# Twelve of sixteen macro tiles as a loop of six turns, and other shares of the copies, in a rotation of an 8192 x 8192 matrix

## The chip, the cores and the metric

The kernel runs on one NeuronCore of a Trainium2 chip. The metric is the device time of one execution in microseconds (us). Before the change the median of three runs is 1258.31 us (1258.22 to 1258.31).

The core has five engines with instruction streams of their own: TensorE (PE in the profile; PEld is its weight load), VectorE (DVE), ScalarE (ACT), GpSimd (POOL) and SyncE (SP). They meet through semaphores. Data moves between the chip's main memory (HBM) and the on-chip memory (SBUF, 128 partitions) on 16 DMA engines, which all queues share. TensorE writes to a second on-chip memory, PSUM, from which ScalarE copies here.

## The reference

```python
def setup_inputs():
    return {"x": np.random.randn(8192, 8192).astype(np.float32), "k": 1}

def reference(x, k):
    return np.rot90(x, k)
```

With k = 1 this is out[8191 - c, r] = x[r, c]: a transposition with the order of the columns reversed. Every one of the 67,108,864 values is read once and written once, 268.4 MB each way, and nothing is calculated.

## The kernel before

**Tiles.** x is cut into KK = 16 macro tiles of R = 1024 rows and W = 4096 columns. A macro tile comes in as T = 8 loads of 128 rows x 4096 columns (2 MB, 16 KB to a partition). It goes out as J = 8 outputs of 512 rows of the result x 1024 columns (2 MB). So there are 128 loads m, counted through, and 128 outputs n = 8 kk + j. A load consists of 8 chunks of 128 x 512, one for each output; output j needs chunk j of all eight loads of its macro tile.

**Buffers.** There are five buffers of 128 x 4096: LAND = 2 for loads, OUTS = 3 in which outputs are put together. The first five loads go to all five at once. Between them lies `ring`, with 63 chunk slots (SLOTS): a chunk of the next macro tile is written where an output of the present one has just been read. Therefore VectorE may take load m only when output m - 8 has been read from the ring. The 64th chunk of a macro tile, the corner, has no slot: it is turned around inside its landing buffer (L354), transposed by TensorE (L393) and copied by ScalarE (L433).

**Two ways to make an output.** Which outputs go which way is said by `by_pe(kk)` (L84): all eight in the first and last macro tile, j = 0 and 4 (BY_PE) in macro tiles 1 to 13, and five in macro tile 14.
- By TensorE: VectorE copies the chunk into the ring with its columns reversed (L359, COPY). TensorE transposes 32 blocks of 128 x 128 into two PSUM halves (L407), and ScalarE copies these into the output buffer (L449).
- By quadrants: VectorE's 32 x 32 block transpose writes the chunk into the ring (L359, STREAM_TRANSPOSE). Each 32 x 32 block then still has to go to another group of 32 partitions. Since an engine's copy takes one group of 32 partitions to one other, an output takes 16 copies of 32 x 1024 (`moves`, L245). BY_DVE = 1 of the 16 is made by VectorE (L341), BY_POOL = 9 by GpSimd (L324), the other 6 by ScalarE (L430 and L439). GpSimd's last copies wait until ScalarE and VectorE have made theirs, and ScalarE then waits for GpSimd.

**Order.** Each engine's whole program is written out by hand, with the waits, by a function: `by_gpsimd` (L303), `by_sync` (L327), `by_vector` (L331), `by_tensor` (L372), `by_scalar` (L416). Everything is unrolled.
- SyncE issues the loads (three and four halves of the first ten are ScalarE's), each when its landing buffer has been taken.
- For load m VectorE first makes its copy for output m - 8, if that goes by quadrants; then it waits for the landing and for output m - 8; then it takes the chunks.
- ScalarE goes through the outputs in order of n. It makes its part, waits for the others' and issues the store (L457). So a late output also holds the store of the next one.
- `room_for(wait, n)` (L180) waits until the last store from the buffer of output n has landed. Before the change that buffer is the one of output n - 3 (`out_buf`, L161).

Of the kernel before, what the change touches and what calls it, by code (L numbers as in the profile page):

```python
# [6 lines left out]
P = 128  # L7
# [6 lines left out]
J = W // (G * P)  # L14
# [5 lines left out]
SLOTS = T * J - 1  # L20

Q = 32
BY_DVE = 1
BY_POOL = 9
BY_PE = [0, 4]
EARLY = range(T + 2)
BOTH = EARLY[-4:]

# [3 lines left out]
LAND = 2  # L32
OUTS = 3

LINE = 1024
HEAD = 224


def whole_reads(nc):

    for fn in nc.m.functions:
        for block in fn.blocks:
            for n, ins in enumerate(block.instructions):
                if not isinstance(ins, mybir.InstDMACopy):
                    continue
                src = ins.ins[0]
                ap = [list(d) for d in src.ap]
                if len(ap) == 3 and ap[2][0] == 1 and ap[1][0] == ap[2][1]:
                    ap = [ap[0], [1, 1], [1, ap[1][1] * ap[2][1]]]
                    block.instructions[n] = copy.replace(  # L50
                        ins,
                        ins=[copy.replace(src, ap=ap)],
                        ant_dge_precooked=False,
                    )


def slot(kk, t, j):
# [4 lines left out]
def kernel(tc: tile.TileContext, x: bass.AP, k: bass.AP, out: bass.AP):  # L62
    nc = tc.nc
# [6 lines left out]
    KK = len(macros)  # L70
# [26 lines left out]
    for n, (kk, ts, js, blocks) in enumerate(outs):  # L97
        if moved[n]:
            continue
        rows = len(ts) * P  # L100
# [25 lines left out]
    def moved_until(n):  # L126
        return sum(moved[: n + 1])
# [28 lines left out]
    def load_buf(m):  # L156
        if m < T:
            return m % (LAND + OUTS)
        return LAND + 2 if m == T else (m - T - 1) % LAND

    def out_buf(n):  # L161
        e = n - (KK * J - J)
        if e < 0:
            return LAND + (n + 1) % OUTS
        ends = [load_buf(n_load - 2)]
        ends += [LAND + (KK * J - J + i + 1) % OUTS for i in range(OUTS)]
        ends += [load_buf(n_load - 1)]
        return ends[e % len(ends)]

    def once(e):  # L170
        seen = {}

        def wait(sem, n):
            if seen.get(sem, 0) < n:
                seen[sem] = n
                e.wait_ge(sem, n)

        return wait
# [33 lines left out]
    for m in range(n_load):  # L212
        kk, t = divmod(m, T)
# [49 lines left out]

    pairs = [(a, q) for a in range(P // Q) for q in range(P // Q)]

    def load(e, m):
        r0, c0 = macros[m // T]
        b = load_buf(m)
        rows = slice(0, P)
        if m in BOTH:  # L270
            rows = slice(0 if e is nc.sync else 1, P, 2)
        r = r0 + m % T * P
        e.dma_start(  # L273
            out=bufs[b][rows, :], in_=x[r : r + P, c0 : c0 + W][rows, :]
        ).then_inc(s_land[b], 16)

    def queues(m):
        if m in BOTH:
            return [nc.sync, nc.scalar]
        return [nc.scalar if m in EARLY and m % 2 else nc.sync]  # L280

    def load_in_turn(e, m):
        if e not in queues(m):
            return
        last = [i for i in range(m) if load_buf(i) == load_buf(m)]
        taken(e.wait_ge, last[-1])
        load(e, m)

    def landings(m):
        return 16 * sum(1 + (i in BOTH) for i in range(m + 1) if load_buf(i) == load_buf(m))  # L290
# [5 lines left out]
    with tc.tile_critical():  # L296
        for m in range(LAND + OUTS):
            for e in queues(m):
                load(e, m)
    tc.close()  # L300
    tc.compile()  # L301

    def by_gpsimd(e):  # L303
        e.memset(ident, 0.0).then_inc(s_id, 1)  # L304
        e.wait_ge(s_id, 1)
        e.affine_select(  # L306
            out=ident,
            in_=ident,
            compare_op=mybir.AluOpType.not_equal,
            fill=1.0,  # L310
            base=0,
            pattern=[[-1, P]],
            channel_multiplier=1,
        ).then_inc(s_id, 1)
        wait = once(e)
        for n, (kk, _, js, _) in enumerate(outs):
            if moved[n]:
                room_for(wait, n)
                wait(s_rev, turned_in(n))
                others = {BY_POOL - 2: s_act, BY_POOL - 1: s_dve}  # L320
                for c, (to, of) in enumerate(moves(n, pairs[BY_DVE : BY_DVE + BY_POOL])):
                    if c in others:
                        wait(others[c], moved_until(n))
                    i = e.tensor_copy(out=to, in_=of)  # L324
                i.then_inc(s_pool, 1)

    def by_sync(e):  # L327
        for m in range(LAND + OUTS, n_load):
            load_in_turn(e, m)

    def by_vector(e):  # L331
        wait = once(e)
        for m in range(n_load):
            kk, t = divmod(m, T)
            b = load_buf(m)
            n = m - T
            if n >= 0 and moved[n]:
                room_for(wait, n)
                wait(s_rev, turned_in(n))
                for to, of in moves(n, pairs[:BY_DVE]):  # L340
                    i = e.tensor_copy(out=to, in_=of)  # L341
                i.then_inc(s_dve, 1)
            e.wait_ge(s_land[b], landings(m))
            if n >= 0:
                if moved[n]:
                    e.wait_ge(s_pool, moved_until(n))  # L346
                else:
                    e.wait_ge(s_half, turned_until(n))
            for js in pieces[m]:
                if (m, js[0]) == (n_load - 1, J - 1):  # L350
                    e.wait_ge(s_half, turned_until(KK * J - J))
                if kk < KK - 1 and (t, js[0]) == (T - 1, J - 1):
                    wait(s_rev, rev[m, 0])
                    e.tensor_copy(  # L354
                        out=at(bufs[b][:], 0, [[CH, 1], [1, CH]]), in_=landed(b, js)
                    ).then_inc(s_rev, 1)
                    continue
                turn = e.transpose if in_quadrants(kk, js[0]) else e.tensor_copy
                turn(out=chunk(kk, t, js), in_=landed(b, js)).then_inc(s_rev, 1)  # L359
# [10 lines left out]
                yield n, parts[n]  # L370

    def by_tensor(e):  # L372
        wait = once(e)
        e.wait_ge(s_id, 2)
        used = {}
        for n, some in in_turn():
            kk, ts, js, blocks = outs[n]
            rows = len(ts) * P
            order = [(part, f) for part in some for f in part[2]]
            if js[0] == 0 and kk < KK - 1:  # L380
# [33 lines left out]
                    used[h] = part  # L414

    def by_scalar(e):  # L416
        wait = once(e)
        e.wait_ge(s_id, 2)
        e.copy(scratch, ident[:, :1])  # L419
        for m in EARLY[LAND + OUTS :]:  # L420
            load_in_turn(e, m)
        for n, (kk, ts, js, blocks) in enumerate(outs):
            r0, c0 = macros[kk]
            rows = len(ts) * P
            b = out_buf(n)
# [16 lines left out]
            else:  # L442
                for k, h, cols in parts[n]:
# [11 lines left out]
            top = M - c0 - js[0] * CH - groups * P  # L455
            left = r0 + ts[0] * P
            e.dma_start(  # L457
                out=out[top : top + groups * P, left : left + rows].rearrange(
                    "(g m) f -> m g f", m=P
                ),  # L460
                in_=bufs[b][:, : groups * rows].rearrange("m (g f) -> m g f", f=rows),
            ).then_inc(s_store[b], 16)

    by_gpsimd(nc.gpsimd)
    by_sync(nc.sync)
    by_vector(nc.vector)
    by_tensor(nc.tensor)
    by_scalar(nc.scalar)

    last = {out_buf(n): n for n in range(n_out)}  # L470
    for b in sorted(last, key=last.get):
# [36 lines left out]
```

## Time and profile before

| what | before |
|---|---|
| median of three runs | 1258.31 us |
| span of the profiled execution (its own time, first to last instruction) | 1256.9 us |
| busy: TensorE / VectorE / ScalarE / GpSimd | 330.0 / 612.7 / 682.5 / 805.0 us |
| GpSimd's copies L324 | 729, 804.3 us |
| ScalarE's copies of quadrants L430 and L439 | 486, 497.7 us |
| VectorE's copies of quadrants L341 | 81, 108.0 us |
| transposes on TensorE L407 and L393 | 1,556 |
| moved by DMA, HBM read and written | 537.22 MB, 268.44 and 268.44 MB |
| mean rate over the span | 427 GB/s |
| a macro tile in the middle of the span | 78.1 us |

The span is that of one profiled execution; the runs' times include what lies around it. Lines such as L324 are lines of the kernel's file. In a row of the groups of instructions stand the line, the engine, the operation, what is written and read with partitions x elements, the count, the busy time and the mean of one in ns, and then the idle time of the engine ahead of these instructions with what ended it. In the DMA queue rows stand packets, MB, and the time of the packets as a share of 16 engines' span; the queues called "instruction" carry the engines' code. A row of the table of stretches has for each of the five engine columns the busy us and the number of instructions, then TensorE's granted clock, the mean share of the 16 DMA engines that was busy, and the rate.

### The profile page before, as it was taken

The numbers are of one execution on the slowest core, as the hardware profiler recorded it, in microseconds if no ns is written. First come the engines' busy times: TensorE is split into PE (matmuls) and PEld (weight loads), VectorE is DVE, ScalarE is ACT, GpSimd is POOL, SyncE is SP. The second block draws the span as 40 slices with busy tenths as digits, with TensorE's granted clock in tenths as the row PEclk, the third lists the DMA queues.
The fourth block names the chain that finished last, engine by engine and source line by source line (L and its number), as shares of the span: only waits on it lengthen the run. The fifth ranks groups of instructions, "written<-read, shape, count | busy, mean of one in ns | idle before, by whom it ended". The sixth has DMA issues, their size and how long they took to land.

```text
span 1256.9 us, 5389 instructions
## 1 busy us (share of the span) xinstructions
PE 330.0 (26%) x1556; PEld 267.9 (21%) x1556; DVE 612.7 (49%) x373; ACT 682.5 (54%) x637; POOL 805.0 (64%) x735
## 2 busy tenths in 40 slices
PE   1555122221122211222212322023220232214374
PEld 0444111211112110121201212012120121103364
DVE  2544554556545555455555555555555555453310
ACT  0334565565555655566555555556555655556454
POOL 0000886768867679677797767977678776795500
PEclk9987555555555555565555555555555555555588
DMA  9999999999999999999999999999999999999999
GB/s 398 420 431 428 430 428 430 430 430 430 428 429 430 430 429 428 430 429 430 429 430 429 430 427 431 430 430 429 430 429 430 429 429 429 429 430 429 430 426 394
DMA packets 36957, 537.22 MB, mean 427 GB/s; under 512 B 4160, under 2 KB 4160, under 8 KB 4160
## 3 DMA queue, kind: packets, MB, share of 16 engines
q10 hardware_dynamic: 19184, 278.93, 52.2%
q1 hardware_dynamic: 17744, 257.96, 48.0%
q8 instruction: 12, 0.20, 0.1%
q14 instruction: 17, 0.14, 0.0%
HBM read 268.44 MB, written 268.44 MB: 427 GB/s over the span
## 4 chain that ended last, share of the span: by engine, by line
DMA 72%; DVE 16%; POOL 5%; ACT 3%; issue 2%; PE 1%; ACTq 0%; SPq 0%; DVEq 0%
DMA buf<-in_x_dram 65%; DVE ring L359 16%; DMA out_dram<-buf 7%; POOL buf L324 5%; ACT buf L449 3%; PE ps L407 1%; ACTq L457 0%; DVE buf L341 0%; PE ps L393 0%; SPq L273 0%; DVE buf L354 0%; DVEq L346 0%; SPq L301 0%; SPq L193 0%; SPq L296 0%
## 5 line engine op out<-in xcount | busy, mean ns | idle before, releaser
L324 POOL COPY buf<-ring 32x1024 f32<-32x1024 f32 (+1 forms) x729 | 804.3, 1103 | 380.3 <-DMA out_dram<-buf 343.4
L407 PE MATMUL ps<-head,ring 128*128 128x128 f32 x1496 | 316.8, 384 | 880.6 <-DVE ring L359 430.3
L407 PEld LDWEIGHTS ps<-head,ring 128*128 128x128 f32 x1496 | 257.6, 200 | 936.9 <-DVE ring L359 435.0
L359 DVE COPY ring<-buf 128x1024 f32<-128x1024 f32 (+5 forms) x152 | 158.1, 1047 | 599.3 <-DMA buf<-in_x_dram 578.1
L439 ACT COPY buf<-ring 32x1024 f32<-32x1024 f32 (+1 forms) x405 | 414.8, 1024 | 4.9
L359 DVE STREAM_TRANSPOSE ring<-buf 128x3072 f32<-128x3072 f32 (+2 forms) x125 | 357.8, 2870 | 0.0
L449 ACT COPY buf<-ps 128x2048 f32<-128x2048 f32 (+1 forms) x134 | 174.6, 1355 | 251.8 <-PE ps L407 177.1
L430 ACT COPY buf<-ring 32x1024 f32<-32x1024 f32 x81 | 82.9, 1024 | 291.6 <-POOL buf L324 229.9
L341 DVE COPY buf<-ring 32x1024 f32<-32x1024 f32 x81 | 108.0, 1334 | 0.0
L393 PE MATMUL ps<-head,buf 128*128 128x128 f32 x60 | 16.2, 424 | 30.3 <-DVE buf L354 30.3
L393 PEld LDWEIGHTS ps<-head,buf 128*128 128x128 f32 x60 | 10.6, 213 | 35.7 <-DVE buf L354 35.7
L433 ACT COPY buf<-ps 128x512 f32<-128x512 f32 x15 | 8.8, 586 | 8.9 <-DMA out_dram<-buf 8.8
L354 DVE COPY buf<-buf 128x512 f32<-128x512 f32 x15 | 5.8, 388 | 0.0
L419 ACT ACT_TABLE_LOAD x1 | 1.3, 1283 | 3.4 <-PEq L301 3.4
L304 POOL MEMSET head<- 128x128 f32 x1 | 0.2, 205 | 2.9 <-POOLq L301 2.9
L306 POOL TENSOR_SCALAR_AFFINE_SELECT head<-head 128x128 f32<-128x128 f32 x1 | 0.3, 292 | 0.2 <-POOL head L304 0.2
L489 POOL MEMSET const-float32-0.0<- 128x1 f32 x1 | 0.1, 98 | 0.2 <-issue 0.2
L419 ACT COPY head<-head 128x1 f32<-128x1 f32 x1 | 0.2, 192 | 0.0
L489 POOL MEMSET const-bfloat16-1.0<- 128x1 bf16 x1 | 0.1, 100 | 0.0
L489 POOL MEMSET const-uint8-127<- 128x1 uint8 x1 | 0.1, 100 | 0.0
L489 POOL MEMSET const-float32-1.0<- 128x1 f32 x1 | 0.1, 98 | 0.0
## 6 DMA issues: line engine op xcount, KB each, us to landing
out_dram<-buf ACTq DMA_DIRECT2D x128, 2048.0 KB, 18.6
buf<-in_x_dram SPq DMA_DIRECT2D x121, 2048.0 KB, 15.2
buf<-in_x_dram ACTq DMA_DIRECT2D x3, 2048.0 KB, 17.3
buf<-in_x_dram SPq DMA_DIRECT2D x4, 1024.0 KB, 16.1
buf<-in_x_dram ACTq DMA_DIRECT2D x4, 1024.0 KB, 16.5
```

Of the source, the lines that this page charges most:

```text
L324: i = e.tensor_copy(out=to, in_=of)
L341: i = e.tensor_copy(out=to, in_=of)
L354: e.tensor_copy(out=at(bufs[b][:], 0, [[CH, 1], [1, CH]]), in_=landed(b, js)).then_inc(s_rev, 1)
L359: turn(out=chunk(kk, t, js), in_=landed(b, js)).then_inc(s_rev, 1)
L393: i = e.transpose(corner[:, g * P : g * P + P], bufs[load_buf(m)][:, g * P : g * P + P], ident,)
L407: i = e.transpose(ps[h][:, to : to + P], chunk(kk, t, [j])[:, 0, off : off + P], ident,)
L419: e.copy(scratch, ident[:, :1])
L430: e.copy(to, of)
L433: e.copy(at(bufs[b][:], rows - P, [[rows, G], [1, P]]), at(corner, 0, [[P, G], [1, P]]),).then_inc(s_freed, 1)
L439: i = e.copy(to, of)
L449: e.copy(at(bufs[b][:], cols[0], [[rows, deep], [1, run]]), at(ps[h][:], 0, [[run, deep], [1, run]]),).then_inc(s_ev, 1)
L489: nc = _bacc.Bacc("TRN2", target_bir_lowering=False, num_devices=1)
```

## The change

1. TensorE makes outputs 0, 2, 4 and 6 of macro tiles 1 to 13 instead of 0 and 4. Of the 16 copies of each other output GpSimd makes 12 instead of 9, VectorE 2 instead of 1, ScalarE 2 instead of 6.
2. The engines' programs are first recorded as lists of operations, by macro tile. For GpSimd (macro tiles 1 to 12), VectorE and TensorE (2 to 13) two macro tiles after each other become the body of a loop of six turns. Within it a wait for a count that grows from turn to turn compares with a register that is worked out from the turn's number. ScalarE and SyncE stay unrolled; so do the macro tiles outside the loops.
3. So that every second macro tile uses the same buffers, the output buffers follow the lists TURN, in turn for even and odd macro tiles.
4. On GpSimd both waits for the other engines' copies stand ahead of its last copy; an increment of a semaphore, `passed`, which nobody waits for, follows waits in the loop.

```diff
-BY_DVE = 1
-BY_POOL = 9
-BY_PE = [0, 4]
+BY_DVE = 2
+BY_POOL = 12
+BY_PE = [0, 2, 4, 6]
...
+TURN = [[1, 2, 0, 1, 2, 0, 1, 2], [1, 0, 2, 1, 0, 2, 1, 0]]
...
+class Program:
...
+    def play(self, nc, e, first=None, times=0):
+        span = range(first, first + 2 * times) if times else range(0)
+        for kk, ops in self.parts.items():
+            if kk not in span:
+                for op in ops:
+                    op.run(e)
+            elif kk == first:
+                self.loop(nc, e, first, times)
+
+    def loop(self, nc, e, first, times):
+        turns = [
+            [op for kk in (first + 2 * i, first + 2 * i + 1) for op in self.parts[kk]]
+            for i in range(times)
+        ]
...
+        with nc.Fori(1, times + 1, engines=[e.engine]) as i:
+            passed = nc.alloc_semaphore("passed") if e is nc.gpsimd else None
+            waited = False
+            for ops in zip(*turns):
+                op = ops[0]
+                if waited and op.name != "wait_ge" and passed is not None:
+                    e.sem_inc(passed, 1)
+                waited = op.name == "wait_ge"
+                if op.name == "wait_ge":
+                    n = [o.args[1] for o in ops]
+                    step = n[1] - n[0]
+                    assert n == [n[0] + k * step for k in range(times)]
+                    assert n[0] > 0 and step >= 0
+                    op.run(e, value=i * step + (n[0] - step) if step else n[0])
+                    continue
...
+                    op.run(e)
...
     def out_buf(n):
         e = n - (KK * J - J)
         if e < 0:
-            return LAND + (n + 1) % OUTS
+            return LAND + TURN[n // J % 2][n % J]
         ends = [load_buf(n_load - 2)]
-        ends += [LAND + (KK * J - J + i + 1) % OUTS for i in range(OUTS)]
+        ends += [LAND + i for i in range(OUTS)]
...
-                others = {BY_POOL - 2: s_act, BY_POOL - 1: s_dve}
                 for c, (to, of) in enumerate(moves(n, pairs[BY_DVE : BY_DVE + BY_POOL])):
-                    if c in others:
-                        wait(others[c], moved_until(n))
+                    if c == BY_POOL - 1:
+                        wait(s_act, moved_until(n))
+                        wait(s_dve, moved_until(n))
                     i = e.tensor_copy(out=to, in_=of)
...
-    by_gpsimd(nc.gpsimd)
     by_sync(nc.sync)
-    by_vector(nc.vector)
-    by_tensor(nc.tensor)
-    by_scalar(nc.scalar)
+    for e, by, first, times in (
+        (nc.gpsimd, by_gpsimd, 1, 6),
+        (nc.vector, by_vector, 2, 6),
+        (nc.tensor, by_tensor, 2, 6),
+        (nc.scalar, by_scalar, None, 0),
+    ):
+        program = Program()
+        by(program)
+        program.play(nc, e, first, times)
```

In the changed program GpSimd has about 27 instructions ahead of its loop, 129 in the body and 93 behind it; VectorE 47, 88 and 67; TensorE, with two instructions for a transpose, about 789, 575 and 833. ScalarE has 489 instead of 783.

## The prediction

> **What bounds the kernel now.** I read the profile's page first: the slices and the DMA queues.
>
> ```profile
> span 1256.9 us, 5389 instructions
> ...
> DMA  9999999999999999999999999999999999999999
> ...
> q10 hardware_dynamic: 19184, 278.93, 52.2%
> q1 hardware_dynamic: 17744, 257.96, 48.0%
> q8 instruction: 12, 0.20, 0.1%
> q14 instruction: 17, 0.14, 0.0%
> ```
>
> No slice of the DMA row is below 9, and the loads and stores alone take 52.2 + 48.0 = 100.2% of the 16 DMA engines. The compute engines are 21 to 64% busy and wait. So the time is the time of the DMA engines. The two instruction queues look negligible; they are not, which the table of stretches shows for the last microseconds (columns: stretch, length, five engines, clock, DMA share, GB/s).
>
> ```profile
> 1252.00:1253.00 1.00, 0.00 (x0) 0.00 (x0) 0.00 (x0) 0.00 (x0) 0.00 (x0) 0.50 1.00 426
> 1253.00:1253.50 0.50, 0.00 (x0) 0.00 (x0) 0.00 (x0) 0.00 (x0) 0.00 (x0) 0.50 0.70 295
> 1253.50:1254.00 0.50, 0.00 (x0) 0.00 (x0) 0.00 (x0) 0.00 (x0) 0.00 (x0) 0.50 0.85 360
> 1254.00:1254.50 0.50, 0.00 (x0) 0.00 (x0) 0.00 (x0) 0.00 (x0) 0.00 (x0) 0.50 0.31 131
> ...
> 1255.00:1255.50 0.50, 0.00 (x0) 0.00 (x0) 0.00 (x0) 0.00 (x0) 0.00 (x0) 0.50 0.54 229
> 1255.50:1256.00 0.50, 0.00 (x0) 0.00 (x0) 0.00 (x0) 0.00 (x0) 0.00 (x0) 0.50 0.24 98
> ```
>
> Until 1253 all sixteen are full; then they stop one after another, over more than 3 us. All carry the same share of every transfer, so some were delayed. The trace's packet records say by what. Each DMA engine is a chain of 16 KB packets of 0.611 to 0.615 us without a gap, and now and then an instruction packet stands in it. There are 17 of 8 KB after the start (q14, 0.309 us each) and 12 of 16 KB (q8, 0.95 to 1.04 us). Followed through, a chain falls behind the freest one by about 0.6 us at each 8 KB packet and about 1.35 us at each 16 KB one. Three chains carry nearly all the 8 KB packets, and each chain's come when one particular engine has run another 120 to 140 instructions: GpSimd's six on one (at 137, 332, 528, 722, 918, 1114 us; lag at the end 3.8 us, so 0.63 each), ScalarE's six on another, VectorE's four on a third; the one left is SyncE's. TensorE's twelve come every 256 instructions and go round about eight further chains. Four chains without instruction packets end some 3.4 us before the last. So code comes in blocks of about 128 instructions, 256 on TensorE. One fetch comes for each block that an engine enters, and TensorE runs over the boundaries without a pause, so it is the following block that is fetched.
>
> So: span = 1253.1 us + lag of the most delayed chain; before 1253.1 + 3.8 = 1256.9. The median is 1258.31, 1.4 us above this execution's span; I add 1.4 at the end.
>
> **The change, part by part.** For the copies the rows by shape:
>
> ```profile
> L324 POOL COPY buf<-ring 32x1024 f32<-32x1024 f32 x612 | 686.7, 1122 | 375.2 <-DMA out_dram<-buf 343.4 <-DVE buf L341 7.3
> ...
> L359 DVE STREAM_TRANSPOSE ring<-buf 128x3072 f32<-128x3072 f32 x91 | 306.0, 3363 | 0.0
> ...
> L449 ACT COPY buf<-ps 128x2048 f32<-128x2048 f32 x52 | 96.5, 1867 | 228.7 <-PE ps L407 154.1 <-POOL buf L324 73.9 <-ACT buf L449 0.7
> L341 DVE COPY buf<-ring 32x1024 f32<-32x1024 f32 x68 | 95.9, 1411 | 0.0
> L359 DVE COPY ring<-buf 128x1024 f32<-128x1024 f32 x91 | 88.3, 970 | 422.4 <-DMA buf<-in_x_dram 405.4 <-POOL buf L324 13.7 <-PE ps L407 3.2
> ```
>
> The DMA issues (copies, KB each, median us from issue to landing):
>
> ```profile
> out_dram<-buf ACTq DMA_DIRECT2D x128, 2048.0 KB, 18.6
> buf<-in_x_dram SPq DMA_DIRECT2D x121, 2048.0 KB, 15.2
> ```
>
> (1) Shares of the copies. Outputs moved by quadrants go from 81 to 55 (13 x 4 + 3). GpSimd fills one in 12 x 1.122 = 13.5 us and about 0.6 of waiting, before 9 x 1.122 = 10.1 and 0.6. ScalarE makes 2 copies for 6. VectorE makes two copies, 2.8 us, and per load one copy and one transpose of 2048 columns each: about 1.74 (the row of 128x2048) + 2.3 (between 1.77 for 1536 and 3.36 for 3072) = 4.0, before 0.97 + 3.36 = 4.3. TensorE and ScalarE fill an output in about 4.3 us (the spacing of issues when nothing else holds them). None of this is on the path as long as the DMA queues hold work. An output buffer comes round every 3 x 9.77 = 29.3 us (78.1 us per macro tile of 8 outputs); a store holds it 18.6, so 10.7 are left for filling. The mean fill is now (14.1 + about 6) / 2 = 10, so the stores can stay as deep: 18.6 us each where 2 MB at 430 GB/s need 4.9. Loads: 15.2 in flight plus 4.0 on VectorE against two periods, 19.5. The backlog of both is over 10 us; I put the cost at nothing. If that cover were gone, a late GpSimd output would hold ScalarE's in-order issue of it and of the next, and VectorE's load eight later.
>
> (2) Buffer order TURN. Output 0 of a macro tile takes the buffer of output 6 before it, two steps back instead of three: 19.5 us for 18.6 of store and 4 to 6 of filling, 3 to 5 us short. But output 0 needs the last load of its macro tile, which VectorE takes only when output 7 is made, some 15 us after 6 was issued; the store of 6 has then 3 to 4 us to go and the last tiles take 4. Lateness under 3 us meets a full store queue. Nothing; its price otherwise is in the rivals.
>
> (3) Waits on registers. A few tens of register instructions per turn on each looped engine; engines wait for the DMA anyway. Nothing, by the same cover.
>
> (4) Code. This is what reaches the path. Counting the instructions of the changed program: ScalarE 489 for 783, not looped, so 4 fetches for 6. GpSimd: about 27 ahead of the loop, a body of 129, 93 after it, executed 892. VectorE: 47, body 88, 67. TensorE: 789, body 575, 833, executed about 5,070 for 3,148. The trace of before has no backward jump, so what a turn costs has to be bounded. From below: nothing, if all blocks of the body stay on the engine; then GpSimd fetches 2 in all. From above: three per turn. GpSimd's body is longer than a block of 128 and lies on two, A and B. The jump enters A, which must come (1), entering A fetches B (2), entering B fetches the block behind it (3). The row nearest is the straight run, where each block entered costs one fetch: two for the two blocks of a turn, three if the jump has to refill both. I take the middle of two and three. GpSimd: 1 in the first turn, 5 jumps x 2.5, 1 behind the loop = 14.5 fetches (12 to 17) x 0.63 = 9.1 us of lag (7.6 to 10.7) on its chain, where there were 3.8. VectorE, whose body straddles the boundary near its 70th instruction, has almost the same on another chain, 11 to 16. TensorE's body lies on three blocks: 3 + 2 + 5 x 4 + 3 = 28 over eight chains, 3.5 x 1.35 = 4.7 us, less than GpSimd's. These lags stand on different chains and don't add. The pause at a jump itself, two packets and a fetch of about 0.6 us each and the way there, is covered as in (1).
>
> [...]
>
> Sum: 1253.1 + 9.1 = 1262.2 us of span, against 1256.9; with 1.4 around it 1263.6 us. Its own range: 12 fetches give 1253.1 + 7.6 + 1.4 = 1262.1, 17 give 1265.2; with half a microsecond for phase 1261.6 to 1265.7.
>
> **The rivals.**
> A, the loop stays on the engine. No jump fetches; GpSimd 2, VectorE 1 or 2, TensorE 3 + 2 + 3 = 8 on eight chains (1.4 to 1.7), ScalarE 4 x 0.6 + 0.3 = 2.7, the last. 1253.1 + 2.7 + 1.4 = 1257.2 us. For it: no row shows a block fetched a second time. Against it: nothing in before jumps back, so none could be, and one fetch for every block entered, from the first to the last, is how a small buffer looks.
> [...]
>
> B, transfers run dry. If output 0 waits out the store of output 6 (the 3 to 5 us of (2)) and GpSimd's 14.1 us follow at once, both queues can empty once per macro tile. It decides from the point where a stall exceeds the 10 us of backlog; 1 us of empty DMA engines in each of 13 macro tiles is 13 us: 1271 us. For it: GpSimd's fill now exceeds the 10.7 us. Against it: the mean fill does not.
>
> C, clearly faster. The worst chain would have to lag less than 1.3 us: two ScalarE fetches or one of TensorE on any chain. Bound: 1253.1 + 1.3 + 1.4 = 1255.8 us and less, at best 1254.5. ScalarE's four fetches alone speak against it.
>
> **How the numbers follow.** About 0.2% (2.5 us) is what a measurement of this kernel can tell from no change. Forecast 0.62, A 0.25, B 0.06, C 0.07. Slower by over 0.2% is above 1260.8: forecast and B, 0.68. Within: A, 0.25. Faster: C, 0.07. The range reaches from A's 1257.0 to 1266.0, above the forecast's upper bound, and leaves out B and C, 0.13.
>
> **What would show it.** Instruction packets: q14 up from 17 to some 30 or more and q8 from 12 to between 20 and 30 shows (4) right; both down shows A. The share of the DMA engines in the last 10 us should fall off over 7 to 10 us where it was 3. Stretches of 100 us in the middle at 429 to 430 GB/s and DMA 9 in every slice show (1) to (3) right; a digit below 9 there shows B. Wrong outright would be a time below 1256 with as many instruction packets as before, or a slow middle with few of them.

## The result, and the profile after

| | before | after |
|---|---|---|
| median (lowest to highest), six runs each | 1258.27 us (1258.22 to 1258.31) | 1262.12 us (1261.19 to 1264.08) |
| profiled execution: its own time / span | 1258.2 to 1258.3 / 1256.9 us | 1263.2 / 1261.9 us |
| busy: TensorE / VectorE / ScalarE / GpSimd | 330.0 / 612.7 / 682.5 / 805.0 us | 520.6 / 596.8 / 391.0 / 754.2 us |

The ratio is 1.0033, with a 95% interval of 1.0021 to 1.0044: the change makes the kernel 0.33% slower. The forecast was 1263.6 us. The profiled execution of the changed kernel is 1.1 us longer than its median, so what its trace loses is more than the median lost. The time came out as forecast; the cause did not, as the page of the changed kernel shows at once. These are its rows of slices and of DMA queues, of the same form as those shown of before:

```profile
span 1261.9 us, 7238 instructions
...
DMA  9999999999999999999999999999999999999999
GB/s 398 420 428 423 410 430 412 430 429 413 431 427 428 431 430 428 431 431 428 430 431 430 428 430 431 430 428 431 430 428 430 431 430 428 431 430 428 429 421 385
...
q10 hardware_dynamic: 19184, 278.93, 52.0%
q1 hardware_dynamic: 17744, 257.96, 48.1%
q8 instruction: 8, 0.13, 0.0%
q14 instruction: 9, 0.07, 0.0%
```

The forecast rested on more code packets (q8 and q14): there were to be 20 to 30 and 30 or more. There are 8 and 9, fewer than the 12 and 17 of before. What is new stands in the row of GB/s: slices 5, 7 and 10 (410, 412, 413) are 4% low, a slice being 31.5 us. The DMA row still says 9 there. Ten microseconds at a time, the table of stretches of after (columns as in the prediction) shows where the three slices lose:

```profile
120.00:130.00 10.00, 5.80 (x25) 5.00 (x26) 3.81 (x2) 5.78 (x5) 6.81 (x7) 0.50 1.02 378
130.00:140.00 10.00, 6.55 (x32) 5.93 (x31) 5.06 (x5) 3.70 (x3) 1.04 (x1) 0.67 0.97 393
200.00:210.00 10.00, 6.42 (x28) 5.62 (x29) 4.52 (x4) 5.78 (x5) 9.63 (x10) 0.50 1.01 393
210.00:220.00 10.00, 5.65 (x28) 5.02 (x27) 4.97 (x4) 3.70 (x3) 2.42 (x2) 0.67 0.98 403
280.00:290.00 10.00, 7.19 (x32) 6.39 (x33) 5.20 (x4) 5.78 (x5) 9.67 (x9) 0.50 1.01 390
290.00:300.00 10.00, 5.20 (x27) 4.45 (x26) 4.71 (x3) 3.70 (x3) 1.75 (x2) 0.67 0.99 419
700.00:800.00 100.00, 41.56 (x174) 34.88 (x175) 52.03 (x34) 29.27 (x26) 70.55 (x62) 0.57 1.01 430
```

The middle of the span runs at 430. Against that the six stretches lose 1.21 + 0.86 + 0.86 + 0.63 + 0.93 + 0.26 = 4.75 us of transfer; in before the same six run at 428 to 433, of which these are the first two:

```profile
120.00:130.00 10.00, 1.50 (x8) 1.10 (x6) 5.35 (x3) 6.25 (x6) 7.22 (x7) 0.67 1.01 431
130.00:140.00 10.00, 0.00 (x0) 0.00 (x0) 6.20 (x3) 6.25 (x6) 9.65 (x9) 0.50 1.01 430
```

The span has grown by 5.0. The three places are 80 us apart: each is where one macro tile follows another. The DMA engines count as busy there (0.97 to 1.02), so the share does not show the loss, and only the rate does.

What happens at the first of them is in the timeline of after (start, duration, engine, line, operation, in brackets the idle time ahead and what ended it; every line is L102 here, the helper that records the operations):

```profile
122.60 0.69 PE L102 MATMUL ps<-head,ring 128*128 128x128 f32 x2 [9.17 <-DMA out_dram<-buf]
...
123.08 1.06 PE L102 MATMUL ps<-head,buf 128*128 128x128 f32 x4
...
124.23 0.33 SPq L383 DMA_DIRECT2D buf<-in_x_dram  x1
...
126.19 1.96 DVE L102 COPY ring<-buf 128x2048 f32<-128x2048 f32 x1 [9.16 <-PE ps L102]
126.84 0.55 ACTq L102 DMA_DIRECT2D out_dram<-buf  x1
```

Read it from the top. TensorE has stood for 9.17 us, until a store landed. That store is output 6 of the macro tile before, issued at 98.3, and output 0 now takes its buffer (TURN). The chain of waits of after has it as one of its longest pieces, and that of before has nearly the same one (start, duration, what):

```profile
98.33 24.22 DMA out_dram<-buf
```

```profile
97.44 25.04 DMA out_dram<-buf
```

The wait for this landing stands in TensorE's program ahead of output 0, and behind output 0 come the corner's four transposes (the matmuls that read `buf`). SyncE's next load goes into the buffer that holds the corner and waits for them: it is issued at 124.2, where before it was at 117.0. VectorE's next take, at 126.19, also waits for TensorE, 9.16 us. So not only a store is late, a load is too.

In the packet records of 120 to 124 us stand 100 packets of stores and 2 of loads: the load queue has run empty. The stores alone still move 427 to 428 GB/s, so the loss is not there. It comes when the stores are worked off too: from 126 to 132 us stand 109 packets of loads and 8 of stores, at 270 to 354 GB/s. They belong almost all to the load issued at 124.2; the next was issued at 130.4. The 128 packets of that one load take 838 ns on average and up to 2,138, against 611 otherwise (767 and 739 ns on average at the next two places). Loads without stores need not be slow: with several of them on the way, 10 to 20 us of before run at 426 GB/s. Why the packets of a single load take longer is not shown.

The waits of SyncE sum it up (line, waited for, total us, times, longest), first after and then before, L303 and L193 being the same place in the code:

```profile
SPq L303 <- PE ps L102: 164.5, 14, 17.5
```

```profile
SPq L193 <- PE ps L393: 134.6, 14, 10.0
```

Output 0 waits for this store at every one of the 14 boundaries, but not equally long. TensorE stands ahead of the corner for 9.17, 5.34 and 5.24 us at the three places that lose, 4.56 at the fourth and 2.6 to 2.8 at the other ten, where no slice is below 428 GB/s until the last two of the span. The store takes 24.2 us at the first boundary and 20.0 to 20.2 at all later ones. What shortens the wait from the fifth on is TensorE, which comes 17.3 to 17.5 us after the store was issued instead of 14.7 to 15.5. From the timeline of after at 670 us:

```profile
670.65 0.69 PE L102 MATMUL ps<-head,ring 128*128 128x128 f32 x2 [2.57 <-DMA out_dram<-buf]
...
672.27 8.65 SPq L383 DMA_DIRECT2D buf<-in_x_dram  x2
```

The end of the span, in stretches of after:

```profile
1257.00:1258.00 1.00, 0.00 (x0) 0.00 (x0) 0.00 (x0) 0.00 (x0) 0.00 (x0) 0.50 0.92 393
1258.00:1258.50 0.50, 0.00 (x0) 0.00 (x0) 0.00 (x0) 0.00 (x0) 0.00 (x0) 0.50 0.85 360
1258.50:1259.00 0.50, 0.00 (x0) 0.00 (x0) 0.00 (x0) 0.00 (x0) 0.00 (x0) 0.50 0.40 164
1259.00:1260.00 1.00, 0.00 (x0) 0.00 (x0) 0.00 (x0) 0.00 (x0) 0.00 (x0) 0.50 0.12 49
1260.00:1261.00 1.00, 0.00 (x0) 0.00 (x0) 0.00 (x0) 0.00 (x0) 0.00 (x0) 0.50 0.08 33
```

The forecast had the fall stretched from 3 to between 7 and 10 us; it takes some 3.5 and begins 5 us later. By the packet records of the last store the 16 chains end at 1254.79 on average in before and 1259.09 in after (+4.3), the last one 1.65 and 2.34 behind that average (+0.7). So most of the change is time that all 16 lost together.

### The profile page after: what moved, and what is told of

Same layout as the page of the kernel before. It is cut to its first block, busy times and chain, and to the rows that moved or that the text cites. A ratio compares the mean times of both kernels' runs of the same rounds, so it can differ in the third digit from the quotient of the medians.

```text
span 1261.9 us, 7238 instructions
## 1 busy us (share of the span) xinstructions
PE 520.6 (41%) x2388; PEld 436.2 (35%) x2388; DVE 596.8 (47%) x389; ACT 391.0 (31%) x339; POOL 754.2 (60%) x666
## 4 chain that ended last, share of the span: by engine, by line
DMA 75%; DVE 10%; issue 6%; ACT 4%; POOL 2%; PE 1%; ACTq 0%; DVEq 0%; SPq 0%; POOLq 0%
DMA buf<-in_x_dram 63%; DMA out_dram<-buf 12%; DVE ring L102 10%; ACT buf L102 4%; POOL buf L102 2%; PE ps L102 1%; DVE buf L102 1%; ACTq L102 0%; DVEq L99 0%; SPq L383 0%; SPq L411 0%; POOLq L149 0%; SPq L303 0%; POOLq L99 0%; SPq L406 0%
## 5 line engine op out<-in xcount | busy, mean ns | idle before, releaser
L102 POOL COPY buf<-ring 32x1024 f32<-32x1024 f32 (+1 forms) x660 | 753.5, 1142 | 437.6 <-DMA out_dram<-buf 228.3
L102 PE MATMUL ps<-head,ring 128*128 128x128 f32 x2328 | 507.8, 397 | 725.7 <-DMA out_dram<-buf 297.8
L102 PEld LDWEIGHTS ps<-head,ring 128*128 128x128 f32 x2328 | 423.4, 208 | 809.9 <-DMA out_dram<-buf 319.0
L102 ACT COPY buf<-ps 128x512 f32<-128x512 f32 (+3 forms) x227 | 277.8, 1288 | 796.3 <-POOL buf L102 459.9
L102 DVE COPY ring<-buf 128x2048 f32<-128x2048 f32 (+4 forms) x152 | 212.7, 1406 | 620.0 <-DMA buf<-in_x_dram 565.5
L102 DVE STREAM_TRANSPOSE ring<-buf 128x2048 f32<-128x2048 f32 (+1 forms) x112 | 246.3, 2199 | 0.0
L102 DVE COPY buf<-ring 32x1024 f32<-32x1024 f32 (+1 forms) x110 | 147.2, 1338 | 0.7
L102 ACT COPY buf<-ring 32x1024 f32<-32x1024 f32 (+1 forms) x110 | 111.7, 1016 | 57.8 <-DMA out_dram<-buf 47.7
L102 PE MATMUL ps<-head,buf 128*128 128x128 f32 x60 | 15.9, 420 | 0.0
L102 PEld LDWEIGHTS ps<-head,buf 128*128 128x128 f32 x60 | 13.0, 229 | 0.0
L102 DVE COPY buf<-buf 128x512 f32<-128x512 f32 x15 | 5.8, 386 | 0.0
L102 POOL MEMSET head<- 128x128 f32 x1 | 0.2, 204 | 2.9 <-POOLq L411 2.9
L102 POOL TENSOR_SCALAR_AFFINE_SELECT head<-head 128x128 f32<-128x128 f32 x1 | 0.3, 292 | 0.2 <-POOL head L102 0.2
L102 ACT COPY head<-head 128x1 f32<-128x1 f32 x1 | 0.2, 191 | 0.0
## 6 DMA issues: line engine op xcount, KB each, us to landing
out_dram<-buf ACTq DMA_DIRECT2D x128, 2048.0 KB, 15.7
```

Of the source, the lines that this page charges most:

```text
L102: i = getattr(e, self.name)(*self.args, **kwargs)
```

## The experiments

Two theories stood against each other after the result. The first: the rotation TURN makes output 0 wait for a store that is too young, and this is the whole loss. The rivals: the new shares of the copies, or the loops, cost the time. The expectations name their theories themselves. A last group tests the prediction's own model of code packets. All times in this table are medians with the lowest and the highest; before is 1258.2 to 1258.3 in each comparison. A trace shows one execution: in e1, e7, e8 and e10 it is the longest of its series, in e3 the shortest.

| run | shares | rotation | loop | time, us (runs) | ratio to before, 95% |
|---|---|---|---|---|---|
| e1_shares | new | old | no | 1259.55, 1259.24 to 1261.95 (11) | 1.0010, 1.0001 to 1.0019 |
| e2_order | old | TURN | no | 1260.56, 1259.95 to 1261.32 (11) | 1.0018, 1.0009 to 1.0027 |
| e3_unrolled | new | TURN | no | 1260.80, 1260.32 to 1263.45 (7) | 1.0028, 1.0017 to 1.0039 |
| e4_loop_old_shares | old | TURN | yes | 1260.35, 1259.85 to 1261.73 (11) | 1.0018, 1.0009 to 1.0027 |
| e5_body_of_four | new | TURN | 3 turns of 4 | 1263.15 (1) | |
| e6_body_of_six | new | TURN | 2 turns of 6 | 1261.80 (1) | |
| e7_room_on_scalar | new | TURN | yes | 1260.04, 1259.52 to 1261.07 (11) | 1.0014, 1.0005 to 1.0023 |
| e8_tight_elsewhere | new | another | yes | 1260.16, 1259.90 to 1260.82 (10) | 1.0015, 1.0006 to 1.0024 |
| e9_old_shares_room | old | TURN | yes | 1258.53, 1258.01 to 1259.10 (11) | 1.0001, 0.9992 to 1.0010 |
| e10_middle | between | TURN | yes | 1259.29, 1258.98 to 1259.97 (11) | 1.0007, 0.9998 to 1.0016 |
| e11_more_code | old | old | no | 1259.46, 1259.28 to 1259.65 (11) | 1.0009, 1.0000 to 1.0018 |
| e12_sync_code | old | old | no | 1259.78, 1258.88 to 1260.02 (11) | 1.0011, 1.0002 to 1.0020 |

**The parts one by one.** The first run keeps the new shares alone:

```diff
-            return LAND + TURN[n // J % 2][n % J]
+            return LAND + (n + 1) % OUTS
...
-        (nc.gpsimd, by_gpsimd, 1, 6),
-        (nc.vector, by_vector, 2, 6),
-        (nc.tensor, by_tensor, 2, 6),
+        (nc.gpsimd, by_gpsimd, None, 0),
+        (nc.vector, by_vector, None, 0),
+        (nc.tensor, by_tensor, None, 0),
```

> The new shares of the copies alone: everything unrolled, output buffers in plain rotation (n + 1) % 3 as before. Theory T (the buffer order TURN lets output 0 of a macro tile take the buffer of output 6 just before it, two steps back, and this empties the load and store queues at the first macro-tile boundaries, some 4.3 us in all): no stretch below 420 GB/s between 100 and 1180 us; the time then follows the code, TensorE's blocks rise from 12 to 18 or 19, two or three on a chain, 1253.1 + 3 x 1.35 + 0.3 + 1.4 = about 1258.9 us (1258 to 1259.5). Rival R1 (GpSimd's fill of 13.5 us empties the queues, whatever the buffers): stretches of 380 to 415 GB/s at 120, 200 and 280 us and 1262 to 1264 us. Rival R2 (the loop itself, its jumps and register waits, delays the engines): as T.

The median rises by 1.3 us, about a third of the change, to just above the range that T gave. Its profiled execution is the longest of its eleven (1261.95), so its trace overstates the median. In it no slice falls to 413. Its row of slices:

```profile
GB/s 399 422 430 427 422 429 423 430 426 427 431 427 429 431 428 429 429 428 430 429 428 427 428 429 429 429 430 430 427 431 429 428 431 428 428 431 428 429 421 379
```

Slices 5 and 7 (422, 423) are slightly low, and others too: small losses in several places, beside 18 code packets of TensorE for 12. How the 1.3 us divide between the two is not separated. The shares are a part of the loss, not the whole.

The second run has the rotation alone: the diff of the loops above, and the old shares.

```diff
-BY_DVE = 2
-BY_POOL = 12
-BY_PE = [0, 2, 4, 6]
+BY_DVE = 1
+BY_POOL = 9
+BY_PE = [0, 4]
```

> The buffer order TURN alone: unrolled, shares of the copies as before. T: stretches of 380 to 415 GB/s at the first macro-tile boundaries, 2 to 4 us lost: 1260.3 to 1262.3 us; instruction packets as before (12 and 17). R1 and R2: 1258.3 us within 0.3, no such stretch.

The rotation alone costs 2.35 us, and the deep slices are there (5 and 7):

```profile
GB/s 398 418 432 425 412 427 422 430 429 431 428 429 432 427 430 429 428 431 429 429 431 428 430 430 428 431 429 430 430 428 430 429 427 430 428 429 430 429 425 391
```

At 280 us this run has no dip (428 and 428 GB/s). So neither more work on GpSimd nor a loop is needed for the first two dips. The third run has shares and rotation without the loops (only the second hunk of the first diff), the fourth the loops and the rotation with the old shares (only the diff of the second).

> The changed kernel without its loops: new shares and TURN, every engine unrolled. T: the stretches at 120, 200 and 280 us are there as with the loops; with the code's 18 or 19 TensorE blocks 1258.9 + 4.3 = about 1263 us (1262 to 1265). R1: the same, 1262 to 1265 us. R2: no such stretch and 1258 to 1259.5 us.

> Loops and TURN with the shares of before (GpSimd 9 of 16 copies, TensorE two outputs of eight). T: stretches below 415 GB/s at the first boundaries, few instruction packets (5 or 6 of 16 KB): 1257 + 2 to 4 = 1259 to 1261 us. R1: no such stretch, about 1257 us. R2: 1261 to 1263 us, with lost transfer at every turn of the loop, that is every 156 us.

Without loops the time is 1260.80, which neither T (1262 to 1265) nor R2 (1258 to 1259.5) had expected. The interval of the ratio (1.0017 to 1.0039) overlaps that of the changed kernel (1.0021 to 1.0044), and the 1.3 us between the two are within the scatter of both; a cost of the loops of that size with the new shares is neither shown nor excluded. With the old shares the loops cost nothing that these runs can show: 1260.35, where the rotation alone gave 1260.56. The dip at the first boundary comes back in both runs; the second is there in e4_loop_old_shares (390) and not in e3_unrolled, whose stretches are these:

```profile
120.00:130.00 10.00, 6.27 (x28) 5.47 (x29) 4.20 (x4) 5.78 (x5) 7.65 (x7) 0.51 1.05 395
130.00:140.00 10.00, 4.92 (x31) 4.04 (x29) 3.94 (x3) 3.70 (x3) 1.04 (x1) 0.83 0.97 398
200.00:210.00 10.00, 7.91 (x38) 6.47 (x38) 6.17 (x4) 5.78 (x5) 9.31 (x8) 0.59 1.00 424
210.00:220.00 10.00, 3.87 (x19) 3.40 (x19) 3.59 (x3) 4.71 (x4) 2.02 (x2) 0.83 1.02 434
```

So one boundary is struck in this execution, two in those of e2 and e4, three in that of the changed kernel. Whether the shares, the loops or the chance of one execution decides that is open. The stretches of e4_loop_old_shares, to be compared with those of e9_old_shares_room below:

```profile
120.00:130.00 10.00, 6.12 (x25) 4.92 (x25) 4.23 (x3) 6.65 (x6) 3.39 (x4) 0.50 1.02 387
130.00:140.00 10.00, 0.00 (x0) 0.00 (x0) 5.57 (x4) 8.08 (x9) 6.26 (x6) 0.50 0.99 396
```

**Longer loops.** How much code stays on an engine, since in the changed kernel no packet of 16 KB comes from 299 to 1148 us:

```diff
-        span = range(first, first + 2 * times) if times else range(0)
+        span = range(first, first + 4 * times) if times else range(0)
...
-            [op for kk in (first + 2 * i, first + 2 * i + 1) for op in self.parts[kk]]
+            [op for kk in range(first + 4 * i, first + 4 * i + 4) for op in self.parts[kk]]
...
-        (nc.gpsimd, by_gpsimd, 1, 6),
+        (nc.gpsimd, by_gpsimd, 1, 3),
```

VectorE and TensorE likewise; the second run has bodies of six macro tiles and two turns.

> The changed kernel with three turns of four macro tiles instead of six of two: bodies of some 258 instructions on GpSimd, 176 on VectorE and 1,150 on TensorE (4.5 blocks of 256). Theory H (the engines keep several blocks, and a jump back into a kept block fetches nothing): no instruction packet of GpSimd, VectorE or TensorE in the second and third turn; in all about 10 of 16 KB (the code's length, 2,770 / 257) and 10 to 12 of 8 KB after the start. Rival, the prediction's step (each block entered is fetched again once the body is longer than the two blocks that the changed kernel's GpSimd needed): about 20 or more of 16 KB and 18 or more of 8 KB. Time by H as the changed kernel, 1261 to 1264 us.

> Two turns of six macro tiles: bodies of some 387 instructions on GpSimd (on four blocks of 128), 264 on VectorE and 1,725 on TensorE (on seven of 256). H: no instruction packet in the second turn, 13 of 16 KB and 11 to 13 of 8 KB in all. If the engines keep fewer blocks than these bodies need: 16 KB packets all through the second turn (from about 630 us), 19 or more, and 8 KB packets of GpSimd there. Time as the changed kernel, 1261 to 1264 us.

With four macro tiles the body is 258 instructions on GpSimd and 1,150 on TensorE. After TensorE's packet at 444 us none of 16 KB comes until 1125, and none of GpSimd's in the second and third turn: three blocks of GpSimd's and five of TensorE's stay. With six macro tiles GpSimd's body has 387 instructions on four blocks, TensorE's 1,725 on seven. The queue rows of e6_body_of_six:

```profile
q8 instruction: 13, 0.21, 0.1%
q14 instruction: 17, 0.14, 0.0%
```

The 8 KB packets are 17 again, and in the second turn they come after GpSimd's 407th, 413th, 447th, 575th and 703rd instruction: a cluster at the jump, and then one every 128 of GpSimd's (VectorE's count stands at 325, 411 and 496 at the last three). TensorE's 13 come before 584 us and after 1121: none in its second turn. So in these two runs GpSimd kept three blocks (258 instructions) and did not keep four (387); TensorE kept seven (1,725). Each time is of one run, and with the scatter of the rotation they tell nothing of the price.

**The wait in another place.** If the loss comes from TensorE holding the corner, then output 0 may wait as long as it likes, provided that TensorE goes on. ScalarE, which writes the buffer, can do the waiting:

```diff
-                if part == parts[n][0] and f == last[part] and n != FIRST[1]:
-                    room_for(wait, n)
...
-            if moved[n] or n == FIRST[1] or (kk < KK - 1 and js[0] == J - 1):
-                room_for(wait, n)
+            room_for(wait, n)
```

> The changed kernel, but the wait for a free output buffer stands on ScalarE ahead of its copies out of PSUM instead of on TensorE in the middle of the transposes. So TensorE makes output 0 and the corner behind it without waiting for the store of output 6, and VectorE and the loads behind TensorE go on. Theory T with its chain (store of output 6, TensorE's output 0 and corner, VectorE's next load, SyncE's next load): stretches of 428 to 431 GB/s throughout, few instruction packets (8 and 9), the last chain 2.7 us behind: 1257.2 us (1256.8 to 1258). Rival R3 (the two-step reuse starves the stores themselves, wherever the wait stands): stretches below 415 GB/s at 120, 200 and 280 us stay, 1261 to 1264 us.

The stretches of e7_room_on_scalar:

```profile
120.00:140.00 20.00, 11.51 (x53) 10.48 (x54) 8.73 (x6) 9.48 (x8) 8.93 (x8) 0.59 1.01 429
200.00:220.00 20.00, 12.12 (x62) 11.08 (x63) 10.03 (x6) 9.94 (x10) 10.59 (x10) 0.68 1.01 428
280.00:300.00 20.00, 12.06 (x62) 10.85 (x60) 10.06 (x6) 8.86 (x9) 10.64 (x10) 0.72 1.01 429
...
1180.00:1200.00 20.00, 6.60 (x37) 5.96 (x36) 7.93 (x4) 5.61 (x6) 13.36 (x11) 0.59 1.00 407
```

The three dips are gone, although output 0 is still stored late (126.1 us; 126.8 in the changed kernel, 118.0 in before): the load that came at 124.2 now comes at 117.2. That is the mechanism. R3's loss with the stores is not there. But the time misses both expectations: only 2.1 of 3.85 us come back, and not all as T had it. In the profiled execution a new loss of (430 - 407) / 430 x 20 = 1.07 us stands at 1180 to 1200, in the last macro tile but one, and one chain ends 2 us after the next; what causes these was not followed up.

The rotation can also be tight at another output instead of output 0 and 1:

```diff
-TURN = [[1, 2, 0, 1, 2, 0, 1, 2], [1, 0, 2, 1, 0, 2, 1, 0]]
+TURN = [[1, 2, 0, 1, 2, 0, 1, 2], [0, 1, 2, 0, 2, 1, 2, 0]]
```

> The changed kernel with another TURN: even macro tiles 1 2 0 1 2 0 1 2, odd ones 0 1 2 0 2 1 2 0. The plain rotation goes on over every boundary of macro tiles; the two-step reuses are outputs 4 and 6 of the odd macro tiles. T: the stretches at 120, 200 and 280 us go; outputs 4 and 6 have no corner behind them and their data long since, so little is lost there: 1257 to 1259 us. R3: the same loss at the new places (about 160 and 180, 320 and 340 us), 1260 to 1264 us.

The time is above what T gave and inside the range of R3, at its lower end. The stretches at 120, 200 and 280 us are without the dips (428 and more, but for 424 at 210). Small losses stand at places that R3 named: 412 GB/s at 160 to 170 and 415 at 190 to 200, some 0.8 us together. The tight place does not have to be output 0 to cost something; this run doesn't settle more.

With the old shares and the wait on ScalarE, TURN and the loops remain:

```diff
-BY_DVE = 2
-BY_POOL = 12
-BY_PE = [0, 2, 4, 6]
+BY_DVE = 1
+BY_POOL = 9
+BY_PE = [0, 4]
...
-                if part == parts[n][0] and f == last[part] and n != FIRST[1]:
+                if part == parts[n][0] and f == last[part] and n > FIRST[1]:
                     room_for(wait, n)
...
-            if moved[n] or n == FIRST[1] or (kk < KK - 1 and js[0] == J - 1):
+            if n <= FIRST[1]:
                 room_for(wait, n)
```

FIRST[1] is output 1 of the last macro tile: behind it the waits stay on TensorE, everywhere else they are ScalarE's.

> Loops and TURN with the shares of before, and the wait for a free buffer on ScalarE for all but the last seven outputs. T and C: no stretch below 425 GB/s at 120 and 200 us; the loops leave ScalarE's six blocks as they were, so its chain is 3.3 to 3.8 us behind: 1257.8 to 1258.5 us, against 1260.35 with the wait on TensorE. R3: as that, 1260 us.

1258.53, which is before within the interval (0.9992 to 1.0010). In its stretches the dips of e4_loop_old_shares, 387 and 396, are gone:

```profile
120.00:130.00 10.00, 4.87 (x22) 4.47 (x23) 4.43 (x3) 6.52 (x6) 3.62 (x4) 0.50 1.02 434
130.00:140.00 10.00, 1.47 (x12) 1.23 (x10) 5.39 (x4) 8.07 (x9) 6.12 (x6) 0.67 1.00 425
```

So one moved wait takes back 1.8 of the 2.1 us that rotation and loops cost with the old shares. The expectation was met. This run has 7 and 11 code packets (18 in all, 29 in before), and yet the kernel is no faster.

Shares between the two, with the same two hunks on the wait:

```diff
-BY_POOL = 12
-BY_PE = [0, 2, 4, 6]
+BY_POOL = 10
+BY_PE = [0, 3, 6]
```

> A version that could beat both: loops and TURN, TensorE makes outputs 0, 3 and 6, of the other outputs' 16 copies GpSimd 10, VectorE 2, ScalarE 4, and the wait for a free buffer on ScalarE. GpSimd's fill is 10 x 1.12 + 0.6 = 11.8 us, five in 78.1; ScalarE has some 600 instructions, four or five blocks, 2.4 to 3.0 us of lag: 1253.1 + 3.0 + 1.4 = 1257.5 us (1257.0 to 1258.0) if the transfers don't run dry. If GpSimd's fill empties them as with 12 copies: 1259 to 1260 us.

Missed, 1.8 us above what was expected; 1259.29 is in the range that the expectation gave for transfers that run dry. The profiled execution has one dip, 401 GB/s at 1120 to 1130 us, and one chain ends at 1257.59 where the next ends at 1255.85. No version that was run beats before.

**Code packets by themselves.** Two kernels add to the kernel before waits that are met already, which are nothing but code:

```diff
             ).then_inc(s_store[b], 16)
+            for _ in range(4):
+                e.wait_ge(s_id, 2)
```

on ScalarE behind each store (in the trace 256 instructions more), and on SyncE

```diff
             load_in_turn(e, m)
+            for _ in range(3):
+                e.wait_ge(s_id, 2)
```

(three waits behind each load, in the trace 231 instructions more), two blocks in each.

> The kernel before, with four waits after each store on ScalarE that are always met: 255 more ScalarE instructions, two more blocks of 128, nothing else. Theory C (the time is that of the DMA engine that was delayed most, and each 8 KB code packet delays one by 0.6 us; ScalarE's chain ended last): 19 packets of 8 KB for 17, 1258.25 + 2 x 0.6 = 1259.4 us (1259.0 to 1259.8). Rival (code packets slip into gaps, the time is set by the transfers as a whole): 1258.3 us within 0.15; two packets of 0.31 us over 16 engines are 0.04 us.

> The kernel before, with two more instructions (waits that are always met) after each load on SyncE, 234 in all, again two blocks. Theory C: SyncE's code comes over other DMA engines than ScalarE's and GpSimd's, which have lag to spare (under 2.5 us of 3.8): 1258.25 us within 0.2, though the same two packets are added. Rival D (any code packet costs, since the packets of a transfer wait for each other): the same rise as with ScalarE's.

ScalarE's two blocks cost 1.16 us, as expected (1259.4; 1259.46 measured). But by the ends of the chains the last is 1.4 us later than in before, and 0.45 of that is common to all 16 on average. So 0.6 us for each packet on one chain is not shown by this time alone. The queue row of e11_more_code has the two:

```profile
q14 instruction: 19, 0.16, 0.0%
```

The packets that were at 137, 332, 528, 722, 918 and 1114 us are now eight, at 108, 265, 411, 557, 712, 863, 1009 and 1163, while the series at 164, 355, 517, 701, 877 and 1060 stays. The first series is therefore ScalarE's and the second GpSimd's.

SyncE's two cost 1.48 us in the median. Theory C expected nothing, since SyncE's chain was taken to have slack, and missed; the rise is the one that rival D gave. D's reason would delay all chains. In the packet records of e12_sync_code 15 of the 16 chains end at 1253.2 to 1256.4, as in before (1253.0 to 1256.4), and a single one at 1257.63. That is one delayed chain and no common loss: the average end has moved by 0.10 us only. The figure is what two packets of 0.6 us would do on the chain that ended last before (1256.44 + 1.2 = 1257.6). Which engine's packets share a chain could not be followed through the records safely, so the sharing is argued, not shown.

A loop on ScalarE as well wasn't tried; no run shows whether ScalarE's own packets would go with it.

## Why the prediction was right in time and wrong in cause

**(1), shares of the copies, "I put the cost at nothing".** The durations held. GpSimd's twelve copies are 12 x 1.175 = 14.1 us, as worked out with its waiting; VectorE's copy and transpose of 2048 columns are 1.38 + 2.30 = 3.7 for 4.0. From the rows by shape of after:

```profile
L102 POOL COPY buf<-ring 32x1024 f32<-32x1024 f32 x504 | 592.3, 1175 | 360.2 <-DVE ring L102 165.6 <-DMA out_dram<-buf 162.8 <-issue 7.7
...
L102 DVE STREAM_TRANSPOSE ring<-buf 128x2048 f32<-128x2048 f32 x91 | 209.2, 2299 | 0.0
...
L102 DVE COPY ring<-buf 128x2048 f32<-128x2048 f32 x98 | 135.4, 1381 | 490.0 <-DMA buf<-in_x_dram 445.0 <-PE ps L102 23.2 <-POOL buf L102 21.9
```

The cover was not whole: e1 shows 1.3 us, though in it 6 more code packets of TensorE may have a part. The backlog of the store queue, the median from issue to landing, fell from 18.6 to 15.7 us in the changed kernel (16.6 with the shares alone, 16.4 with the rotation alone):

```profile
out_dram<-buf ACTq DMA_DIRECT2D x128, 2048.0 KB, 15.7
buf<-in_x_dram SPq DMA_DIRECT2D x121, 2048.0 KB, 15.8
```

**(2), the order TURN, "Lateness under 3 us meets a full store queue. Nothing".** This is the step behind the measured loss. Two things in it were wrong. The store was taken at the median of 18.6 us, while the chain of waits of before held a row of 25.04 us for this very store, output 6 of the first macro tile; with 24.2 us the wait is 9.17 us. At the later boundaries this store takes 20.0 to 20.2, still more than the median, and the wait is 5.3 us at the second. Under 3 us was right for ten of the 14 boundaries, and there nothing is lost. And the step asked only who stores late. It did not ask what stands behind the waiting instruction on TensorE: the corner, hence the landing buffer, hence a load. The loss comes when the late load goes alone. e2 (the rotation alone, +2.35 us) shows that the rotation costs, and e9 against e4 (-1.8 us for the moved wait, and the dips gone) that it costs through the wait on TensorE. Rival B had the mechanism, "If output 0 waits out the store of output 6", but priced it at once per macro tile for 13 macro tiles and let it start only above 10 us of backlog. In the profiled execution it strikes clearly at three boundaries, for 2.07, 1.49 and 1.19 us (the pairs of stretches above).

**(3), waits on registers, nothing.** No run shows a cost: e4 against e2 is -0.2 us, within both intervals. With the new shares the changed kernel is 1.3 us above e3, and there a cost is not excluded.

**(4), code, "two for the two blocks of a turn, three if the jump has to refill both".** Wrong. No run shows the 2.5 fetches per jump of the sum; that a jump back into a body on two blocks fetches them again was the author's estimate. What the runs showed in its place is that the changed kernel's loop bodies stayed on the engines: from TensorE's packet at 299 us to 1148 none of 16 KB comes, and the 8 KB packets fall from 17 to 9. Of the longer bodies one on three blocks of GpSimd's (258 instructions, e5) did not fetch again, one on four (387, e6) did, and one on seven of TensorE's (1,725, e6) did not. Rival A described this part; its lag of 2.7 us behind the freest chain is close to the 2.9 measured.

The assignment of chains was wrong too: the six packets given to GpSimd were ScalarE's (e11). It changed nothing in the forecast's arithmetic of six packets and 3.8 us of lag.

**The floor and the most delayed chain.** The prediction adds the lag of the most delayed chain to the end of the freest, 1253.1 us. By the packet records the freest chain ends at 1253.0 in before and 1258.6 in after, and the last one at 1256.45 and 1261.43. So both terms failed: the floor, taken as unchanged, rose by 5.6 us, of which 4.75 stand in the six stretches; the lag, forecast to rise by 5.3, fell from 3.4 to 2.9. The 3.8 us of the prediction took in the 0.45 between the last packet and the end of the span, so six packets in 3.4 us are 0.57 each and not 0.63. That a few packets on one chain set the end is argued: e11's time agrees (0.58 for each of two), but part of it is common to all chains, and e12's agrees only if SyncE's packets were on the last chain.

**Sum.** Forecast were +5.3 us from code packets (9.1 for 3.8) and nothing else. Measured are +3.85 in the median and +5.0 in the profiled execution, there +5.6 from the floor and -0.6 from the lag. Two errors, 5.9 us too much for the code and 5.6 us too little for the rotation with the shares, cancelled out. That the time was right is luck.

## What to carry to other kernels

When a buffer is to be used again sooner, take the longest transfers that hold it, not the median, and follow what stands behind the waiting instruction on its engine to the next transfer that it holds back; put the wait on the engine that writes the buffer. In a kernel that is bound by DMA look at the rate by slice: the busy share stayed at 0.97 to 1.02 where 12% of the rate was missing. A right time with a mark that fails, here the code packets, is to be taken as a wrong prediction.

## What the runs showed of the hardware that was not expected

- Loop bodies of 258 instructions on GpSimd (e5) and of 1,725 on TensorE (e6) were not fetched again in later turns; one of 387 on GpSimd (e6) was, in its second turn. Sizes in between were not run.
- At the first place the empty load queue cost nothing as long as stores were queued: they moved 427 to 428 GB/s alone at 120 to 124 us. The loss came when one load was on the way alone: 270 to 354 GB/s at the first place, its packets at the three places 0.74 to 0.84 us on average and up to 2.14 for the same 16 KB, against 0.611. The DMA engines count as busy meanwhile (0.97 to 1.02 in the six stretches of 10 us).
- Fewer code packets brought no time: e9 with 18 is as fast as before with 29. ScalarE's six were not looped; that their chain is among the last in before, and that they set the end, is argued.
- The kernel before scatters by 0.1 us in six runs and by 0.6 to 1.1 in 21 to 33; the kernels with TURN by 0.9 to 3.1 us in 7 to 11, the changed one by 2.9 in six.
